# PEER sub-layer of a DeepNorm decoder layer: all first-table chunks before one pass over the second table, and the gate scatter as one fp32r product per token

## The chip, the cores and the metric

The kernel runs on one core of a Trainium2 chip, as one launch. The metric is the device time of an execution in microseconds (us). Each kernel was executed several times, and the median is given. One execution was also recorded by the hardware profiler, with the start and duration of each engine's instructions and DMA packets.

Engines are named as the profile names them: PE is TensorE (matrix products), PEld its weight loads, DVE is VectorE, ACT is ScalarE, SP is the sync engine, whose queue issues all loads and stores of this kernel. Every engine works off its own instructions in a fixed order.

## The reference, cut to what matters

One decoder layer over 256 tokens of width 2048, in fp32. A modulated layer norm, an attention mixture and an output projection come first; this change leaves them alone. The second sub-layer is PEER: each token scores two sets of 128 sub-keys with 8 heads, keeps 16 of the 128 x 128 pairs a head, and sums those 128 experts out of 16,384.

```python
def peer(h, w_pq, sub_key_1, sub_key_2, u_table, v_table):
    ...
    idx = i1 * PEER_N_KEYS + i2          # 8 heads x 16 experts per token
    g = jax.nn.softmax(vals, axis=-1)
    ...
        u = u_table[it]
        a = jnp.einsum('td,tkd->tk', ht, u)
        w = jax.nn.gelu(a.astype(jnp.float32), approximate=False).astype(ht.dtype) * gt
        return jnp.einsum('tk,tkd->td', w, v_table[it])

def reference(...):
    ...
        ffn = peer(h, w_pq[l], sub_key_1[l], sub_key_2[l], u_table[l], v_table[l])
        x = layer_norm(DN_ALPHA * x + g2 * ffn, ln2_g[l], ln2_b[l])
```

## The kernel before

The kernel gathers nothing. It computes the products with all 16,384 experts for all 256 tokens, applies GELU, multiplies by a dense gate matrix (zero where a token did not choose an expert) and multiplies by the whole second table. Both tables are streamed from HBM, 128 MB each.

Precision: an fp32 operand is split into `hi` (fp32r) and `lo` (the rest, fp32r), and a product is made of three fp32r products (`hi*hi`, `hi*lo`, `lo*hi`). `piece` (L92) loads one 1 MB piece of a table into one of three `raw` buffers by an SP queue DMA, and makes two half pieces: ACT casts `hi` (L98), DVE subtracts `lo` (L100). There are four `hi` and four `lo` buffers, so two pieces can stand ready ahead of PE. `prepare` asks for a piece ahead of its use.

The PEER part runs in stages, by the time of the profile:

- about 565 to 996 us: `u_chunk` (L781) for chunks 0 to 15 of the first table U. A chunk is four pieces and 512 experts. Per piece PE does 16 pairs of one matmul of 512 columns (L132, `hi_u` against `act` hi and lo together) and one of 256 (L133, `lo_u`). Every two pieces ACT and DVE add two PSUM banks into the chunk's `W` tile (L791, L792), and ACT applies GELU (L793). After each piece `pull(PULL_U[c])` lets the expert choice go on by a budget: `axis_top` and `pair_top` find the chosen experts on DVE, and `scatter` (L905) builds the gate matrix.
- about 996 to 1341 us: `v_half(0, 0)` multiplies W of chunks 0 to 15 with the matching rows of the second table V, into eight PSUM banks; the sums go to `y`.
- about 1341 to 1707 us: `u_chunk` for chunks 16 to 31, with the last `w_ada` rows and the residual beside it.
- about 1707 to 2054 us: `v_half(1, LATE)`. The last six rows of V come last, bank by bank, so that the last norm can start on finished columns.

The gate scatter, per token: a one-hot row of the first index, `o1`, and a one-hot row of the second index times the gate, `o2`, both fp32; their outer product sum is a 128 x 128 gate block:

```python
nc.vector.tensor_scalar(o2, iota, i2T[:, t:t + 1], gT[:, t:t + 1], op0=ALU.is_equal, op1=ALU.mult)
nc.tensor.matmul(ps[:, q * P:(q + 1) * P], o1[:, q, :], o2, start=True, stop=True)
```

Four tokens make a group and fill one PSUM bank, which ACT copies into `stg` (L928); every 16 tokens `stg` (1 MB) goes to DRAM as `g_d`. PE carries one fp32 matmul as two records of 128 columns. A group of `scatter` builds `o1` on ACT (four `Abs`, one `Relu`, L919 and L921) or on DVE (L917) by the list `on_vector`: none of four groups for tokens 0 to 127, two of four for tokens 128 to 255.

`v_weights(c)` (L983) loads the gates of two chunks (`gl`, 1 MB in runs of 512 bytes), multiplies W by them on DVE (L989) and splits the product into `whi` and `wlo` (L157, L158). There are 16 W buffers, so all 16 chunks of a half stay in SBUF.

The order on each engine is not that of the code alone: the framework sets it when the program is built, from priorities and its own durations. So the text below shows it from the built programs.

## Time and profile before

| | us |
|---|---|
| median of 3 runs (2072.44 to 2072.8) | 2072.49 |
| the profiled execution | 2069.06 |
| its span, first to last instruction | 2067.3 |
| PE busy in the span | 1999.3 (97%) |
| DVE busy | 1433.5 (69%) |
| ACT busy | 1027.1 (50%) |
| DMA queue of SP, share of 16 engines | 64.9% |

The table is from the head of the profile page. A matmul's record is longer than its distance to the next, since matmuls overlap in the array; so the cost of matmuls on PE's path is read from the starts of successive ones. Idle time of an engine is put down to what ended it. The DMA share is the mean busy share of the core's 16 DMA engines.

### The profile page before, as it was taken

The numbers are of one execution on the slowest core, as the hardware profiler recorded it, in microseconds if no ns is written. First come the engines' busy times: TensorE is split into PE (matmuls) and PEld (weight loads), VectorE is DVE, ScalarE is ACT, GpSimd is POOL, SyncE is SP. The second block draws the span as 40 slices with busy tenths as digits, with TensorE's granted clock in tenths as the row PEclk, the third lists the DMA queues.
The fourth block names the chain that finished last, engine by engine and source line by source line (L and its number), as shares of the span: only waits on it lengthen the run. The fifth ranks groups of instructions, "written<-read, shape, count | busy, mean of one in ns | idle before, by whom it ended". The sixth has DMA issues, their size and how long they took to land.

```text
span 2067.3 us, 26814 instructions
## 1 busy us (share of the span) xinstructions
PE 1999.3 (97%) x10328; PEld 1671.3 (81%) x10329; DVE 1433.5 (69%) x2510; ACT 1027.1 (50%) x1481; POOL 0.2 (0%) x4
## 2 busy tenths in 40 slices
PE   6999998989999999999999999999999999999997
PEld 3567686769988888998888888888888888888886
DVE  7589988889799677676765454477776555445457
ACT  2323457444554778876444444454444454444441
POOL 0000000000000000000000000000000000000000
PEclk8999999989999999999999999999999999999999
DMA  9788877858545555556985555578876656555552
GB/s 368 310 328 337 328 306 277 334 224 325 186 159 191 199 208 197 212 203 225 287 282 188 199 184 203 186 270 307 295 285 245 226 205 237 190 201 186 201 203 102
DMA packets 100865, 496.13 MB, mean 240 GB/s; under 512 B 7793, under 2 KB 41729, under 8 KB 42881
## 3 DMA queue, kind: packets, MB, share of 16 engines
q1 hardware_dynamic: 100736, 494.41, 64.9%
q8 instruction: 81, 1.33, 0.2%
q14 instruction: 48, 0.39, 0.1%
HBM read 473.40 MB, written 20.98 MB: 239 GB/s over the span
## 4 chain that ended last, share of the span: by engine, by line
PE 90%; DVE 7%; ACT 1%; DMA 1%; issue 1%; SPq 0%; DVEq 0%; ACTq 0%
PE u_ps L132 23%; PE u_ps L133 11%; PE v_ps L137 11%; PE v_ps L139 11%; PE v_ps L138 11%; PE win_ps L330 3%; PE g_ps L927 3%; DVE ada L208 2%; PE win_ps L138 2%; PE win_ps L139 2%; PE win_ps L137 1%; PE wo_ps L139 1%; PE wo_ps L138 1%; PE wo_ps L137 1%; PE wpq_ps L137 1%; PE wpq_ps L139 1%
## 5 line engine op out<-in xcount | busy, mean ns | idle before, releaser
L132 PE MATMUL u_ps<-act,hi_u 128*128 128x512 f32 x2048 | 726.5, 399 | 3.0 <-DVE W L792 3.0
L133 PE MATMUL u_ps<-act,lo_u 128*128 128x256 f32 x2048 | 573.6, 280 | 0.0
L100 DVE TENSOR_TENSOR lo_v<-raw_v,hi_v 128x1024 fp32r<-128x1024 f32 x244 | 297.9, 1224 | 263.4 <-ACT hi_v L98 263.3
L132 PEld LDWEIGHTS u_ps<-act,hi_u 128*128 128x128 f32 x2048 | 385.5, 188 | 94.8 <-DVE W L792 3.3
L100 DVE TENSOR_TENSOR lo_u<-raw_u,hi_u 128x1024 fp32r<-128x1024 f32 x256 | 312.2, 1222 | 179.2 <-ACT hi_u L98 178.6
L98 ACT CAST hi_v<-raw_v 128x1024 fp32r<-128x1024 f32 x244 | 257.2, 1054 | 327.8 <-PE v_ps L139 321.3
L133 PEld LDWEIGHTS u_ps<-act,lo_u 128*128 128x128 f32 x2048 | 387.1, 189 | 0.0
L137 PE MATMUL v_ps<-hi_v,whi 128*128 128x512 f32 x976 | 379.7, 389 | 0.0
L138 PE MATMUL v_ps<-lo_v,whi 128*128 128x512 f32 x976 | 379.7, 389 | 0.0
L139 PE MATMUL v_ps<-hi_v,wlo 128*128 128x512 f32 x976 | 379.7, 389 | 0.0
L98 ACT CAST hi_u<-raw_u 128x1024 fp32r<-128x1024 f32 x256 | 267.5, 1047 | 206.5 <-PE u_ps L132 187.0
L208 DVE SCALAR_TENSOR_TENSOR ada<-ada,cb 128x1024 f32<-128x1024 f32 x192 | 229.1, 1219 | 13.8 <-DMA ada<-in_w_ada_dram 13.5
L139 PEld LDWEIGHTS v_ps<-hi_v,wlo 128*128 128x128 f32 x976 | 183.2, 188 | 38.3
L138 PEld LDWEIGHTS v_ps<-lo_v,whi 128*128 128x128 f32 x976 | 183.2, 188 | 37.9
L137 PEld LDWEIGHTS v_ps<-hi_v,whi 128*128 128x128 f32 x976 | 183.2, 188 | 37.9
L925 DVE TENSOR_SCALAR o<-iota,i2T,gT 128x128 f32<-128x128 f32 x256 | 72.9, 342 | 20.0 <-PE g_ps L927 19.9
L330 PE MATMUL win_ps<-raw_win,hmod 128*128 128x512 f32 x192 | 85.6, 601 | 1.2 <-ACT hmod L301 1.2
L137 PE MATMUL wpq_ps<-act,hi_wpq 128*128 128x256 f32 x256 | 73.5, 290 | 2.3 <-ACT act L157 2.1
L791 ACT COPY W<-u_ps 128x256 f32<-128x256 f32 x128 | 47.2, 369 | 52.0 <-PE u_ps L133 51.6
L139 PE MATMUL wpq_ps<-act,lo_wpq 128*128 128x256 f32 x256 | 72.5, 285 | 0.5 <-DVE lo_wpq L100 0.5
L138 PE MATMUL wpq_ps<-act,hi_wpq 128*128 128x256 f32 x256 | 72.9, 286 | 0.0
L330 PEld LDWEIGHTS win_ps<-raw_win,hmod 128*128 128x128 f32 x192 | 36.3, 193 | 42.8 <-issue 41.0
(320 smaller groups left out, 2313.8 us busy)
## 6 DMA issues: line engine op xcount, KB each, us to landing
raw_u<-in_u_dram SPq DMA_DIRECT2D x128, 1024.0 KB, 4.8
raw_v<-in_v_dram SPq DMA_DIRECT2D x122, 1024.0 KB, 4.8
ada<-in_w_ada_dram SPq DMA_DIRECT2D x96, 1024.0 KB, 6.4
raw_win<-in_w_in_dram SPq DMA_DIRECT2D x32, 1024.0 KB, 8.9
raw_wo<-in_w_o_dram SPq DMA_DIRECT2D x16, 1024.0 KB, 6.8
raw_wpq<-in_w_pq_dram SPq DMA_DIRECT2D x16, 1024.0 KB, 6.5
g_d<-stg SPq DMA_DIRECT2D x16, 1024.0 KB, 4.9
gl<-g_d SPq DMA_DIRECT2D x16, 1024.0 KB, 6.7
```

The source lines that it names most:

```text
L98: nc.scalar.copy(hi, raw[:, 2 * j:2 * j + 2, :])
L100: nc.vector.tensor_sub(lo, raw[:, 2 * j:2 * j + 2, :], hi.bitcast(F32))
L132: nc.tensor.matmul(pss[e], hi[:, i, es], act[:, k], start=first and j == 0 and i == 0, stop=False)
L133: nc.tensor.matmul(pss[e][:, 1], lo[:, i, es], act_hi[:, k, :], start=False, stop=last and j == 1 and i == 3)
L137: nc.tensor.matmul(o, sh, mh, start=start, stop=False)
L138: nc.tensor.matmul(o, sh, ml, start=False, stop=False)
L139: nc.tensor.matmul(o, sl, mh, start=False, stop=stop)
L208: nc.vector.scalar_tensor_tensor(w[:, z, :], w[:, z, :], 1.0, cb[:, z * 1024:(z + 1) * 1024], op0=ALU.mult, op1=ALU.mult, accum_out=(modc, ...
L330: nc.tensor.matmul(ps[th], act[:, i, ts], src[:, i, :], start=i == 0, stop=i == 3)
L791: nc.scalar.copy(ws[:, e], pss[e][:, 1])
L925: nc.vector.tensor_scalar(o2, iota, i2T[:, t:t + 1], gT[:, t:t + 1], op0=ALU.is_equal, op1=ALU.mult)
L927: nc.tensor.matmul(ps[:, q * P:(q + 1) * P], o1[:, q, :], o2, start=True, stop=True)
```

## The change

**Order of the stages.** All 32 U chunks run first, then one pass over V in the order `V_ORDER`: chunks 24 to 31, then 0 to 23. The V sums stay in the eight PSUM banks for the whole pass; `y` goes, and the residual is taken from `x1` at the end. The last `w_ada` rows, the reload of `x1` and the rows of the last norm are moved from the second U loop into the V pass (or ahead of it).

**W through DRAM.** There are 8 W buffers (`RING`). Each of chunks 0 to 23 is stored to `w_d` after its GELU (512 KB, SP queue) and loaded again four chunks ahead of its use in the V pass. Chunks 24 to 31 stay.

**Scatter.** `gT` holds each gate as hi and lo in fp32r. `o1` is fp32r, `o2` holds the hi and the lo row side by side, and each token is one fp32r matmul of 256 columns. A group of four tokens needs two banks and two ACT copies. `stg` and `g_d` double (2 MB per 16 tokens); `v_weights` loads both halves and adds them on DVE. `o1` and `o2` of a group are made by whole-group DVE instructions with broadcast operands. DVE builds `o1` for one of four groups throughout.

**Budget.** `PULL_U` is 1.75 a piece for all chunks, and the costs that a group counts are 2.6 (with `o1` on DVE) or 1.9. So a chunk of four pieces pulls 7.0, or 7.0 / ((2.6 + 3 x 1.9) / 4) = 3.4 groups once the expert choice is done.

```diff
-PULL_U = (2.32, 2.23, 1.88, 1.67, 1.83, 2.15, 2.15, 2.41, 2.57, 2.53, 2.28, 2.75, 2.72, 3.19, 2.79, 3.42)
+RING = 8
+SPILL = 32 - RING
+V_ORDER = tuple(range(SPILL, 32)) + tuple(range(SPILL))
+PULL_U = 1.75
...
-    g_d = dram.tile([16, P, NKEY, 16], F32, name="g_d")
+    g_d = dram.tile([16, P, 2, NKEY, 16], F32, name="g_d")
+    w_d = dram.tile([SPILL, P, 4, T], F32, name="w_d")
...
-            return back.tile([P, 4, T], F32, tag=f"W{c % 16}", name=name)
+            return back.tile([P, 4, T], F32, tag=f"W{c % RING}", name=name)
...
+                    if kg == 0 or s < 63:
                         after = s + kg, 1 - kg
                         prepare(a["u"][after], "u{}_{}".format(*after))
+                    else:
+                        prepare(a["v"][4 * V_ORDER[0]], f"v{V_ORDER[0]}_0")
...
-                        pull(PULL_U[c])
+                        pull(PULL_U)
+            if c < SPILL:
+                nc.sync.dma_start(w_d[c], W[c])
...
-            gT = sel.tile([P, T], F32, name="gT")
+            gT = sel.tile([P, T, 2], F32R, name="gT")
...
-                nc.vector.tensor_copy(gT[:, ts], ps[:, 2 * P:3 * P])
+                nc.vector.tensor_copy(gT[:, ts, 0], ps[:, 2 * P:3 * P])
+                nc.vector.tensor_sub(gT[:, ts, 1], ps[:, 2 * P:3 * P], gT[:, ts, 0].bitcast(F32))
...
             def scatter(th, on_vector):
 
                 for tb in range(8 * th, 8 * th + 8):
-                    stg = sel.tile([P, NKEY, 16], F32, tag="stg", name=f"stg{tb}", bufs=2)
+                    stg = sel.tile([P, 2, NKEY, 16], F32, tag="stg", name=f"stg{tb}", bufs=2)
                     for b in range(4):
-                        ps = bank(("sm", "tr")[b % 2], f"g_ps{tb}_{b}")
-                        o1 = sel.tile([P, 4, P], F32, tag="o1", name=f"o1_{tb}_{b}", bufs=2)
+                        t0 = tb * 16 + b * 4
+                        four = slice(t0, t0 + 4)
+                        shp = [P, 4, P]
+                        io = iota.unsqueeze(1).broadcast_to(shp)
+                        o1 = sel.tile(shp, F32R, tag="o1", name=f"o1_{tb}_{b}", bufs=2)
                         vec = b in on_vector
-                        for q in range(4):
-                            t = tb * 16 + b * 4 + q
-                            if vec:
-                                nc.vector.tensor_scalar(o1[:, q, :], iota, i1T[:, t:t + 1], None, op0=ALU.is_equal)
-                            else:
-                                nc.scalar.activation(o1[:, q, :], iota, AF.Abs, bias=i1n[:, t:t + 1])
-                        if not vec:
-                            nc.scalar.activation(o1, o1, AF.Relu, bias=1.0, scale=-1.0)
-                        for q in range(4):
-                            t = tb * 16 + b * 4 + q
-                            o2 = sel.tile([P, P], F32, tag="o2", name=f"o2_{t}", bufs=4)
-                            nc.vector.tensor_scalar(o2, iota, i2T[:, t:t + 1], gT[:, t:t + 1], op0=ALU.is_equal,
-                                                    op1=ALU.mult)
-                            nc.tensor.matmul(ps[:, q * P:(q + 1) * P], o1[:, q, :], o2, start=True, stop=True)
-                        nc.scalar.copy(stg[:, :, b * 4:(b + 1) * 4], ps.rearrange("p (t i) -> p i t", t=4))
-                        yield 1.9 if vec else 1.1
+                        if vec:
+                            nc.vector.tensor_tensor(o1, io, i1T[:, four].unsqueeze(2).broadcast_to(shp), op=ALU.is_equal)
+                        else:
+                            dist = sel.tile(shp, F32, tag="dist", name=f"dist{tb}_{b}", bufs=1)
+                            for q in range(4):
+                                nc.scalar.activation(dist[:, q, :], iota, AF.Abs, bias=i1n[:, t0 + q:t0 + q + 1])
+                            nc.scalar.activation(o1, dist, AF.Relu, bias=1.0, scale=-1.0)
+                        eq = sel.tile(shp, F32, tag="eq", name=f"eq{tb}_{b}", bufs=1)
+                        nc.vector.tensor_tensor(eq, io, i2T[:, four].unsqueeze(2).broadcast_to(shp), op=ALU.is_equal)
+                        o2 = sel.tile([P, 4, 2, P], F32R, tag="o2", name=f"o2_{tb}_{b}", bufs=2)
+                        both = [P, 4, 2, P]
+                        nc.vector.tensor_mul(o2, eq.unsqueeze(2).broadcast_to(both),
+                                             gT[:, four, :].bitcast(F32).unsqueeze(3).broadcast_to(both))
+                        for j in range(2):
+                            ps = bank(("sm", "tr")[j], f"g_ps{tb}_{b}_{j}")
+                            for q in range(2):
+                                nc.tensor.matmul(ps[:, q * T:(q + 1) * T], o1[:, 2 * j + q, :],
+                                                 o2[:, 2 * j + q].rearrange("p z n -> p (z n)"), start=True, stop=True)
+                            t = b * 4 + 2 * j
+                            nc.scalar.copy(stg[:, :, :, t:t + 2], ps.rearrange("p (t z i) -> p z i t", t=2, z=2))
+                        yield 2.6 if vec else 1.9
                     nc.sync.dma_start(g_d[tb], stg)
...
-            later = puller(itertools.chain(axis_top(3), pair_top(0), mixed(pair_top(1), scatter(0, ()), 0.9),
-                                           scatter(1, (1, 3))))
-            for c in range(16):
+            later = puller(itertools.chain(axis_top(3), pair_top(0), mixed(pair_top(1), scatter(0, (1,)), 0.9),
+                                           scatter(1, (1,))))
+            for c in range(32):
                 u_chunk(c, later)
             later(1e9)
...
+            g2w = base.tile([P, 4, D], F32, tag="act", name="g2w")
...
+            def w_load(j):
+                c = V_ORDER[j]
+                if c < SPILL:
+                    W[c] = w_tile(c, f"Wl{c}")
+                    nc.sync.dma_start(W[c], w_d[c])
...
             def v_weights(c):
                 if c % 2 == 0:
-                    gates[0] = val.tile([P, 16, 8, 16], F32, tag="gl", name=f"gl{c}", bufs=1)
-                    nc.sync.dma_start(gates[0], g_d[:, :, 4 * c:4 * c + 8, :].rearrange("b p i t -> p b i t"))
+                    gates[0] = val.tile([P, 2, 16, 8, 16], F32, tag="gl", name=f"gl{c}", bufs=1)
+                    for z in range(2):
+                        nc.sync.dma_start(gates[0][:, z], g_d[:, :, z, 4 * c:4 * c + 8, :].rearrange("b p i t -> p b i t"))
+                    nc.vector.tensor_add(gates[0][:, 0], gates[0][:, 0], gates[0][:, 1])
                 i0 = c % 2 * 4
                 wv = W[c].rearrange("p i (b t) -> p b i t", b=16)
-                nc.vector.tensor_mul(wv, wv, gates[0][:, :, i0:i0 + 4, :])
+                nc.vector.tensor_mul(wv, wv, gates[0][:, 0, :, i0:i0 + 4, :])
...
+            pss = banks8("v_ps")
+            for j, c in enumerate(V_ORDER):
+                if j > 0:
+                    prev = whi, wlo
+                whi, wlo = v_weights(c)
+                if j + 4 < 32:
+                    w_load(j + 4)
+                for i in range(4):
+                    if 4 * j + i >= P - LATE:
+                        continue
+                    for jj, (hi, lo) in enumerate(piece(a["v"][4 * c + i], f"v{c}_{i}")):
+                        for th in range(2):
+                            ts = slice(th * P, (th + 1) * P)
+                            for n in range(2):
+                                mm3(pss[4 * th + 2 * jj + n], whi[:, i, ts], wlo[:, i, ts], hi[:, n, :], lo[:, n, :],
+                                    start=(j == 0 and i == 0), stop=False)
+                if 2 <= j < 18:
+                    m = G2 + j - 2
+                    w = g2w[:, j % 4, :].rearrange("p (z n) -> p z n", z=2)
+                    nc.sync.dma_start(w, a["w_ada"][m].rearrange("p (z n) -> p z n", z=2))
+                    for z in range(2):
+                        nc.vector.scalar_tensor_tensor(w[:, z, :], w[:, z, :], 1.0, cb[:, z * 1024:(z + 1) * 1024],
+                                                       op0=ALU.mult, op1=ALU.mult, accum_out=(modc, modh)[z][:, m:m + 1])
...
+                    nc.sync.dma_start(row_d.rearrange("(c p) -> p c", p=P), modc[:, G2:G2 + 16],
+                                      allow_slow_non_contiguous=True)
+                    bcast_row(g2b, row_d)
+                if j == 20:
+                    for th in range(2):
+                        nc.sync.dma_start(x1[:, th, :], x1_d[th])
+                    for z, nm in enumerate(("ln2_g", "ln2_b")):
+                        bcast_row(rows[:, z, :], a[nm])
...
+            late = base.tile([P, 2, 2, 2, 2, 512], F32R, tag="act", name="late")
...
-                yt = y[:, th]
+                yt = x1[:, th]
...
-                    nc.vector.tensor_add(yt[:, cs], yt[:, cs], tmp)
+                    nc.vector.scalar_tensor_tensor(yt[:, cs], yt[:, cs], ALPHA, tmp, op0=ALU.mult, op1=ALU.add)
```

What the built programs show, row by row (engine's own order; `u27` is step 27 of U, half a chunk, `v27_2` piece 2 of chunk 27; `hi_u29_1_0` is half 0 of piece 1 of step 29).

PE, at the end of a U piece late in the scatter of before; `g_ps13_0` and `g_ps13_1` are two groups of four tokens, of whose eight rows the last five stand here:

```order
L927 MATMUL g_ps13_0_8479<-o2_211_8495,o1_13_0_8480 128x128
L927 MATMUL g_ps13_1_8499<-o2_212_8505,o1_13_1_8500 128x128
L927 MATMUL g_ps13_1_8499<-o2_213_8508,o1_13_1_8500 128x128
L927 MATMUL g_ps13_1_8499<-o2_214_8511,o1_13_1_8500 128x128
L927 MATMUL g_ps13_1_8499<-o2_215_8514,o1_13_1_8500 128x128
L132 MATMUL u_ps27_0_8433<-act_73,hi_u27_1_0_8469 128x512
L133 MATMUL u_ps27_0_8433<-act_73,lo_u27_1_0_8471 128x256
```

PE, at the end of a U piece of the changed kernel (both pieces of step 29 are done); one group of four tokens in two banks:

```order
L135 MATMUL u_ps29_1_7943<-act_73,hi_u29_1_1_7982 128x512
L136 MATMUL u_ps29_1_7943<-act_73,lo_u29_1_1_7984 128x256
L942 MATMUL g_ps5_1_0_8060<-o2_5_1_8058,o1_5_1_8054 128x256 x2
L942 MATMUL g_ps5_1_1_8064<-o2_5_1_8058,o1_5_1_8054 128x256 x2
L135 MATMUL u_ps30_0_8070<-act_73,hi_u30_0_0_8041 128x512
L136 MATMUL u_ps30_0_8070<-act_73,lo_u30_0_0_8043 128x256
```

Four matmuls of 256 columns stand where four (or, with two groups, eight) fp32 matmuls of 128 stood; a group stands at the end of a piece as before.

DVE, where the operands of that same group `5_1` are made in the changed kernel; `W14 <- u_ps28` is the sum of the finished step 28:

```order
L934 TENSOR_TENSOR eq5_1_8056<-iota_3934,i2T_3942 128x512
L103 TENSOR_TENSOR lo_u29_0_0_7912<-raw_u29_0_7908,hi_u29_0_0_7910 128x1024
L103 TENSOR_TENSOR lo_u29_0_1_7916<-raw_u29_0_7908,hi_u29_0_1_7914 128x1024
L103 TENSOR_TENSOR lo_u29_1_0_7980<-raw_u29_1_7976,hi_u29_1_0_7978 128x1024
L798 TENSOR_TENSOR W14_7831<-W14_7831,u_ps28_0_7832 128x256
L927 TENSOR_TENSOR o1_5_1_8054<-iota_3934,i1T_3941 128x512
L103 TENSOR_TENSOR lo_u29_1_1_7984<-raw_u29_1_7976,hi_u29_1_1_7982 128x1024
L798 TENSOR_TENSOR W14_7831<-W14_7831,u_ps28_1_7833 128x256
L937 TENSOR_TENSOR o2_5_1_8058<-eq5_1_8056,gT_3943 128x1024
```

The operands of the group are finished behind the sum of step 28, while PE uses the group behind step 29.

SP, in the first V pass of before, at chunks 2 and 3; `gl` is a gate load:

```order
L82 DMA raw_v2_0_9425<-in_v_dram 128x2048
L986 DMA gl10_10554<-g_d_75 128x16x128
L82 DMA raw_v2_1_9459<-in_v_dram 128x2048
L82 DMA raw_v2_2_9493<-in_v_dram 128x2048
L986 DMA gl12_10838<-g_d_75 128x16x128
```

SP, in the V pass of the changed kernel, at chunks 27 to 29 (the fourth to sixth of its order):

```order
L85 DMA raw_v27_2_12470<-in_v_dram 128x2048
L1012 DMA gl0_13133<-g_d_75 128x16x128
L85 DMA raw_v27_3_12504<-in_v_dram 128x2048
L1042 DMA g2w_11964<-in_w_ada_dram 128x2048
L85 DMA raw_v28_0_12552<-in_v_dram 128x2048
L1006 DMA Wl4_13142<-w_d_76 128x1024
L85 DMA raw_v28_1_12586<-in_v_dram 128x2048
L1042 DMA g2w_11964<-in_w_ada_dram 128x2048
L85 DMA raw_v28_2_12620<-in_v_dram 128x2048
```

Between the V pieces the queue now also carries the second gate half, the stored W and the `w_ada` rows. From the load of `raw_v27_0` to just before that of the first piece of chunk 4 (nine chunks later) the built program has 36 V pieces, 11 gate halves, 10 `w_ada` rows (1 MB each) and 9 W tiles (512 KB).

## Rows read from the trace of the kernel before

**Rows 1.** Two stretches: start:end, length; each engine's busy us; PEclk, DMA share, GB/s
```profile
800.00:979.00 179.00, 179.00 (x1139) 161.53 (x1138) 126.27 (x317) 134.16 (x265) 0.00 (x0) 1.00 0.60 211
...
1715.00:2050.00 335.00, 335.00 (x1480) 277.39 (x1479) 181.61 (x168) 142.76 (x138) 0.00 (x0) 1.00 0.52 188
```

**Rows 2.** The page, engines and costliest groups: busy, mean ns, idle before
```profile
PE 1999.3 (97%) x10328; PEld 1671.3 (81%) x10329; DVE 1433.5 (69%) x2510; ACT 1027.1 (50%) x1481; POOL 0.2 (0%) x4
...
L132 PE MATMUL u_ps<-act,hi_u 128*128 128x512 f32 x2048 | 726.5, 399 | 3.0 <-DVE W L792 3.0
```

**Rows 3.** Groups by line, 600 to 1000 us: busy, mean ns, idle before
```profile
L98 ACT CAST hi_u<-raw_u 128x1024 fp32r<-128x1024 f32 x117 | 122.1, 1047 | 77.7 <-PE u_ps L132 73.6 <-ACT hi_u L98 2.4 <-issue 1.1
L925 DVE TENSOR_SCALAR o<-iota,i2T,gT 128x128 f32<-128x128 f32 x256 | 72.9, 342 | 20.0 <-PE g_ps L927 19.9
L927 PE MATMUL g_ps<-o,o 128*128 128x128 f32 x512 | 66.9, 280 | 0.0
L919 ACT ACTIVATE o<-iota,i1n 128x128 f32<-128x128 f32 x192 | 63.8, 398 | 0.0
...
L928 ACT COPY stg<-g_ps 128x512 f32<-128x512 f32 x64 | 37.4, 585 | 0.4 <-PE g_ps L927 0.4
L921 ACT ACTIVATE o<-o 128x512 f32<-128x512 f32 x48 | 30.2, 629 | 0.8
...
L791 ACT COPY W<-u_ps 128x256 f32<-128x256 f32 x62 | 22.8, 368 | 11.5 <-PE u_ps L133 11.5
L793 ACT ACTIVATE W<-W 128x512 f32<-128x512 f32 x31 | 19.5, 629 | 22.5 <-DVE W L792 22.4
```

**Rows 4.** Groups by line, 1010 to 1330 us, then 1345 to 1690 us
```profile
L989 DVE TENSOR_TENSOR W<-W,gl 128x1024 f32<-128x1024 f32 x10 | 12.1, 1222 | 14.6 <-DMA gl<-g_d 14.6
...
L1031 DVE TENSOR_TENSOR y<-y,cb 128x2048 f32<-128x2048 f32 x2 | 4.6, 2284 | 0.0
```

**Rows 5.** The tail in order of time, after the last matmul
```profile
2055.05 0.69 DVE L1070 TENSOR_TENSOR fin_t<-v_ps,cb 128x512 f32<-128x512 f32 x1 [1.79 <-PE v_ps L139]
```

**Rows 6.** The chain that ended last, its scatter steps: start us, us
```profile
679.10 0.89 PE g_ps L927 x8
685.55 0.89 PE g_ps L927 x8
...
904.30 1.92 PE g_ps L927 x16
911.88 1.92 PE g_ps L927 x16
```

**Rows 7.** Stretches of U without scatter, first and second loop
```profile
600.00:670.00 70.00, 70.00 (x405) 61.19 (x404) 69.35 (x215) 36.04 (x48) 0.00 (x0) 1.00 0.52 184
1350.00:1520.00 170.00, 170.00 (x965) 147.50 (x964) 127.27 (x159) 82.76 (x107) 0.00 (x0) 1.00 0.80 292
```

**Rows 8.** PE in order of time, around eight tokens: start us, us
```profile
830.02 2.08 PE L927 MATMUL g_ps<-o,o 128*128 128x128 f32 x16
831.86 0.48 PE L132 MATMUL u_ps<-act,hi_u 128*128 128x512 f32 x1
832.17 0.28 PE L133 MATMUL u_ps<-act,lo_u 128*128 128x256 f32 x1
```

**Rows 9.** PE in order of time, fp32r matmuls of 256 columns
```profile
559.92 0.28 PE L139 MATMUL wpq_ps<-act,lo_wpq 128*128 128x256 f32 x1
560.04 0.28 PE L137 MATMUL wpq_ps<-act,hi_wpq 128*128 128x256 f32 x1
```

**Rows 10.** The page, DMA issues: KB each, median us to landing
```profile
raw_u<-in_u_dram SPq DMA_DIRECT2D x128, 1024.0 KB, 4.8
...
gl<-g_d SPq DMA_DIRECT2D x16, 1024.0 KB, 6.7
```

**Rows 11.** Two stretches dense with gate traffic, columns as in Rows 1
```profile
1030.00:1062.00 32.00, 32.00 (x143) 26.50 (x142) 21.21 (x19) 13.21 (x14) 0.00 (x0) 1.00 0.85 280
...
979.00:996.00 17.00, 17.00 (x98) 14.76 (x97) 12.36 (x13) 9.64 (x12) 0.00 (x0) 1.00 0.97 309
```

64 lines of the change are left out of this document (15 added, 49 removed).

## The prediction

> **What bounds the kernel now.** I read the page first, then stretches of U and V, then PE in order of time. From the first U chunk on PE is never idle: in a stretch of U with scatter and one of V it is busy for the whole stretch at PEclk 1.00, the 2.4 GHz level [rows 1], and of 2048 pairs of U only one waited, 3.0 us behind a DVE sum [rows 2]. DVE waited 14.6 us for gate loads and ACT for DVE, and PE noticed none of it [rows 3, 4]. So the end of the program is a sum of PE's matmuls, plus the last norm, whose chain starts when DVE, idle for 1.79 us, gets the last bank [rows 5]. The reader should see two things: a matmul taken from PE after 590 us comes off the end at its full start-to-start distance, and work on other engines costs nothing until it makes PE wait.
>
> **Removed: the fp32 scatter matmuls.** In the chain, the steps that hold four tokens (20 of them) come 6.45 us apart, which is a U piece plus the four tokens; the 22 others hold eight [rows 6]. A piece is 16 pairs; 405 records in 70 us make 0.3457 us a pair and 5.53 a piece [rows 7], so four tokens cost 0.92. For eight, PE goes from 830.02 to 831.86, and the pair behind it takes 0.31 from its first to its second start where others take 0.23: 1.84 + 0.08 = 1.92 [rows 8]. Sum: 20 x 0.92 + 22 x 1.92 = 60.6 us for 256 tokens.
>
> **Added: 256 fp32r matmuls of 256 columns.** Before has no scatter matmul of that form. The nearest row is the fp32r product of the query projection, with 256 columns and its own weight load each: 0.12 us apart [rows 9]. 256 x 0.12 = 30.7. From below it is bounded by half a 512-column matmul of V, 335 us / 1480 / 2 = 0.113 [rows 1], or 29.0; from above by the fp32 token's own 0.24, or 61.4, if something in the new form (weights freshly made by ACT or DVE, say) held it there. I take 0.12, because it is the same form on the same engine. **Net: -29.9, bounds -31.6 to +0.8.**
>
> The Trainium skill (TensorE: Matmul & The Clock Gate, section "Wait — 56ns, not 53.3ns?") gives a warm matmul N / 2.4 GHz plus about 2.5 ns, 109 ns for 256 columns. By that the added work would be 28.0 us and the net -32.6. Rows 9 show 120 ns for this form, so page and trace differ here and the trace decides.
>
> **The pace of the pairs.** The second U loop runs at 170 us / 965 records, 0.3523 us a pair, not 0.3457 [rows 7]. I see no cause: same buffers, same clock. Either pace holds for hundreds of pairs. If the 1024 pairs of the second loop ran at the first loop's pace, 6.8 us would go; if the 590 fast pairs or so of the first loop ran at the slow one, 3.8 would come. With a group after most pieces both will be seen, as in the scatter of before. I take -1.5, bounds -6.8 to +3.8.
>
> **Moved at no cost.** The joins between U and V are already dense, so running one V pass instead of two halves gives PE nothing back; eight PSUM banks hold the sums as they did for half. The `y` copies and two DVE sums of 2.28 us [rows 4] leave engines that PE did not wait for. The 3.0 us wait of rows 2 lies where the DVE order is still the same, so I leave it (bounds -3 to +3). The last norm has one scaled sum in place of a sum, 0.69 us as before [rows 5].
>
> **ACT in U.** This is the cover that could go. A chunk needs 8 casts x 1.047 + 4 copies x 0.368 + 2 GELUs x 0.629 = 11.1 us. A group needs three times in four 4 x 63.8 / 192 + 0.629 = 1.96 us, and two copies x 0.585 instead of one: 2.64 [rows 3]. With 3.4 groups a chunk that is 9.0, so 20.1 us of ACT in a chunk that PE takes 64 x 0.349 + 3.4 x 0.48 = 24.0 us for: 84%, against 75% in the stretch from 800 to 979 [rows 1]. It fits. The copy now writes runs of two tokens where it wrote four; no row has that. From below 0.585; from above twice that, 1.17, where ACT just fills the chunk (20.1 + 6.8 x 0.585 = 24.1). I take 0.585, since with runs of four 512 elements cost no more than the contiguous 512 of GELU, 0.629.
>
> **DVE.** A group needs a comparison of 512 elements (0.69 by the nearest row of that size [rows 5]), a product of 1024 (1.22 [rows 4]) and in one of four another comparison: 2.1 us, against at least 4 x 0.342 = 1.37 before [rows 3]. But there is one group a piece, not two. Before, 2.7 us of 7.5; now about 1.8 us of 6. In V it gains 16 sums of 2.28 us and 32 `w_ada` products: per two chunks (43.4 us) 2.28 + 4 x 1.22 = 7.2 us, on 54% [rows 1]; about 71%. Fits.
>
> The new waits: in the DVE order shown, group `5_1` waits for the sum of step 28. Behind that sum stand 0.69 + 1.22 us, the second half of the sum (256 columns, no longer than the 0.69) and 1.22, at most 3.8 us, while PE has two pieces and a group, 11.5 us, before it wants the operands. Some 7.5 us are to spare. On SP, the store of W waits for GELU, and the loads of U pieces queue behind it; they would wait anyway for a `raw` buffer, and a load lands in 4.8 us [rows 10] while five pieces of 5.5 us are buffered ahead.
>
> **DMA in V.** In the nine chunks counted in the SP order there are 61.5 loads of 1 MiB, 64.5 MB, in 9 x 96 x 0.226 = 195 us: 330 GB/s. The queue has not sustained that here. Scaled to a full share, the stretches with gate loads give 280 / 0.85 = 329 and 309 / 0.97 = 319 [rows 11], that with few gives 292 / 0.80 = 365 [rows 7]; gate halves are 18% of the bytes, so I expect about 350 and a share of 0.94. From above, at 319, 202 us would be needed: 7 us of PE waiting. I take +0, as three raw buffers and two split pieces stand ahead.
>
> The Trainium skill (DMA: Bandwidth & Descriptors, section "Specifications") calls 512 bytes enough for line rate. By that a gate half would cost what a V piece does, and the share would be 330 / 365 = 0.90. Rows 10 have 6.7 us to landing against 4.8 for the same bytes, so the trace does not bear it out; the sum is the same.
>
> **Sum.** -29.9 - 1.5 = -31.4 us. The profiled execution of 2069.06 us (span 2067.3 and 1.8 around it) becomes 2037.7. It lay 3.4 us below the median; the median becomes 2072.5 - 31.4 = 2041.1.
>
> **Rivals.**
>
> *Small waits eat part of it.* DMA in the nine chunks (up to 7 us), a late `o2`, late gate sums in DVE's queue. For it: 330 GB/s is beyond what was held for long. Against it: the depth ahead of PE. It gives 2046 to 2062, say 2048. Chance 0.20.
>
> *ACT becomes the bound of U: slower.* The two copies of a group write runs of two elements. If such a copy took 1.76 us (three times the row), ACT would need 20.1 + 6.8 x 1.17 = 28.1 us in a chunk of 24.0, and the 19 chunks that the 64 groups fill would lose 4.1 each, 78 us; with the 31.4 gained, 2119. It decides from about 1.4 us a copy: there the loss is 1.65 us a chunk, 31 in all. Against it: rows 3 show no price of scattered writes. Chance 0.09.
>
> *The matmul is no cheaper.* If the fp32r form took 0.24 us a token, the time is 2072.5 + 0.8 - 1.5 = 2072. Rows 9 speak against it. Chance 0.05.
>
> *More than forecast.* All pairs at the fast pace and the wait of 3.0 us gone: -29.9 - 6.8 - 3.0, 2033 or below. Chance 0.06.
>
> **How the numbers follow.** The forecast, 2034 to 2046, has the remaining 0.60, so 2041. Leaving out 2 in 10, the range is 2033 to 2060: it drops the slower rival, the one without gain, and the far ends. A measurement of this kernel can tell about 0.2%, 4 us, from no change. Faster by more: 0.60 + 0.20 + 0.06 = 0.86; the same 0.05; slower 0.09.
>
> **What would show it.** Right: PE busy for the whole of U and V; scatter matmuls 0.12 us apart, four to a group; copies of 0.6 us; a DMA share near 0.94 early in V. Wrong: gaps in U before scatter matmuls that end with ACT or DVE; `hi` casts that no longer wait for PE (ACT full); gaps in V that end with `raw_v`; scatter matmuls 0.24 us apart.

## The result, and the profile after

The changed kernel takes 2045.01 us, the median of 4 runs (2043.28 to 2047.66), against 2072.64 us of before beside it (2072.44 to 2074.71). The ratio is 0.9872, with a 95% interval of 0.9859 to 0.9885: 27.6 us less, where 31.4 was forecast. The profiled execution took 2044.22 us, with a span of 2042.4.

The head of the page and three of its costliest groups (busy us, mean ns, then idle time of the engine just before them) stand against [rows 2]:

```profile
PE 1973.8 (97%) x10072; PEld 1644.3 (81%) x10072; DVE 1497.3 (73%) x2344; ACT 1048.2 (51%) x1538; POOL 0.2 (0%) x4
...
L136 PE MATMUL u_ps<-act,lo_u 128*128 128x256 f32 x2048 | 575.1, 281 | 0.9 <-DVE lo_u L103 0.9
...
L141 PE MATMUL v_ps<-lo_v,whi 128*128 128x512 f32 x976 | 380.0, 389 | 2.3 <-DVE lo_v L103 2.3
L140 PE MATMUL v_ps<-hi_v,whi 128*128 128x512 f32 x976 | 379.9, 389 | 1.0 <-DVE W L798 1.0
```

PE still sets the end. The 3.0 us wait of [rows 2] is gone, 0.9 us stand in its place, and 3.3 us of waits are new in V, where before had none.

Where the time went is read from PE in order of time (start us, us): the first matmul of U, the first and last of V. The changed kernel, then before, which has two U loops and two V halves:

```profile
574.75 0.40 PE L135 MATMUL u_ps<-act,hi_u 128*128 128x512 f32 x1
...
1328.92 0.40 PE L140 MATMUL v_ps<-hi_v,whi 128*128 128x512 f32 x1
...
2029.72 0.39 PE L142 MATMUL v_ps<-hi_late,wlo 128*128 128x512 f32 x1
```

```profile
571.90 0.40 PE L132 MATMUL u_ps<-act,hi_u 128*128 128x512 f32 x1
...
996.53 0.40 PE L137 MATMUL v_ps<-hi_v,whi 128*128 128x512 f32 x1
...
1344.71 0.39 PE L132 MATMUL u_ps<-act,hi_u 128*128 128x512 f32 x1
...
1706.62 0.40 PE L137 MATMUL v_ps<-hi_v,whi 128*128 128x512 f32 x1
...
2054.62 0.39 PE L139 MATMUL v_ps<-hi_late,wlo 128*128 128x512 f32 x1
```

The differences of these starts give the stages. The same was done for every run below; the label of each run is named again where its experiment is told. All times are us, of one profiled execution each.

| profiled execution | ahead of U | U | V | behind V | span |
|---|---|---|---|---|---|
| before | 571.9 | 424.6 + 361.9 = 786.5 | 348.2 + 348.0 = 696.2 | 12.7 | 2067.3 |
| the changed kernel | 574.8 | 754.2 | 700.8 | 12.7 | 2042.4 |
| again | 574.5 | 751.5 | 701.0 | 12.7 | 2039.7 |
| row_runs | 575.1 | 751.8 | 698.1 | 12.9 | 2037.8 |
| sums_first | 569.9 | 753.5 | 706.5 | 12.7 | 2042.7 |
| rows_and_sums | 574.3 | 751.8 | 696.1 | 12.9 | 2035.0 |
| old_scatter | 574.2 | 776.3 | 702.1 | 12.7 | 2065.3 |
| old_scatter_rows | 574.6 | 776.4 | 696.1 | 12.8 | 2059.9 |
| order_hllh | 574.6 | 750.4 | 700.6 | 12.7 | 2038.3 |
| mends_hllh | 574.3 | 750.9 | 696.8 | 12.9 | 2034.9 |
| mends_hhll | 575.0 | 749.9 | 696.1 | 12.8 | 2033.9 |
| first_pull | 575.2 | 753.8 | 697.4 | 12.7 | 2039.1 |
| mends_small | 574.4 | 753.9 | 698.8 | 12.9 | 2039.9 |
| dense_scatter | 573.7 | 755.0 | 702.0 | 12.8 | 2043.4 |

From before to after: U -32.4, V +4.6, ahead of U +2.9, together -24.8 in the profiled pair. The medians differ by 27.6, and U and V alone make -32.4 + 4.6 = -27.8. That close a fit is partly chance: U of the same changed program was 2.7 us shorter in a second profile (`again`).

The waits of PE by what ended them (us in all, times, the longest), from the first U matmul on, and four stretches of the changed kernel with the columns of [rows 1]: U with scatter, early V, and two pieces of V 10 us long together:

```profile
PE v_ps L141 <- DVE lo_v L103: 2.3, 2, 1.8
PE v_ps L140 <- DVE W L798: 1.0, 2, 0.5
PE u_ps L136 <- DVE lo_u L103: 0.9, 3, 0.5
```

```profile
800.00:979.00 179.00, 179.00 (x1052) 157.74 (x1052) 127.86 (x146) 126.93 (x226) 0.00 (x0) 1.00 0.71 263
...
1400.00:1550.00 150.00, 150.00 (x664) 124.19 (x663) 112.28 (x109) 64.64 (x62) 0.00 (x0) 1.00 0.94 331
```

```profile
1585.00:1590.00 5.00, 5.00 (x23) 4.13 (x22) 5.00 (x5) 1.97 (x2) 0.00 (x0) 1.00 0.82 213
1590.00:1595.00 5.00, 5.00 (x23) 4.13 (x22) 3.87 (x4) 2.62 (x4) 0.00 (x0) 1.00 0.70 49
```

ACT is busy for 126.9 of 179 us in U, 71%, DVE for 112.3 of 150 us in early V, 75%, and the DMA share there is 0.94: the covers held. But in one stretch of 5 us the DMA engines moved 49 GB/s where the 150 us from 1400 us on have 331. SP's queue in order of time has the new write of the g2 modulation row just ahead of it:

```profile
1583.26 0.33 SPq L85 DMA_DIRECT2D raw_v<-in_v_dram  x1
1583.64 0.43 SPq L1048 DMA_DIRECT2D row_d<-modc  x1
1584.12 4.94 SPq L81 DMA_DIRECT2D ln_rows<-in_ln_g_dram  x1
```

This write takes the 2048 values from 128 partitions of 16 columns each, one 4-byte run a value. In the kernel before, `spread_row` had PE transpose them first, in a PSUM bank; in the one V pass all eight banks hold sums. There it was one write of 512-byte runs, and it took 1.4 us to land.

The groups of the scatter by line, 690 to 1240 us (busy us, mean ns, idle before), stand against [rows 3]:

```profile
L937 DVE TENSOR_TENSOR o<-eq,gT 128x1024 fp32r<-128x1024 f32 x64 | 78.3, 1223 | 33.3 <-PE g_ps L942 33.3
L945 ACT COPY stg<-g_ps 128x512 f32<-128x512 f32 x128 | 72.1, 623 | 0.0
...
L942 PE MATMUL g_ps<-o,o 128*128 128x256 f32 x256 | 41.1, 283 | 0.0
```

From the start of one scatter matmul to the next matmul it is 0.120 us on average, 30.8 us in all 256. PE waited for none of them.

At the join of U and V, DVE in order of time (start us, us, in brackets the idle time before and what ended it) and PE's two gaps:

```profile
1328.47 2.29 DVE L1013 TENSOR_TENSOR gl<-gl 128x2048 f32<-128x2048 f32 x1 [2.76 <-DMA gl<-g_d]
1330.68 1.22 DVE L103 TENSOR_TENSOR lo_v<-raw_v,hi_v 128x1024 fp32r<-128x1024 f32 x1
1331.82 0.41 DVE L798 TENSOR_TENSOR W<-W,u_ps 128x256 f32<-128x256 f32 x1
1332.15 1.22 DVE L1016 TENSOR_TENSOR W<-W,gl 128x1024 f32<-128x1024 f32 x1
1333.28 0.41 DVE L798 TENSOR_TENSOR W<-W,u_ps 128x256 f32<-128x256 f32 x1
```

```profile
1332.28 0.50 PE L140 MATMUL v_ps<-hi_v,whi 128*128 128x512 f32 x1 [0.47 <-DVE W L798]
...
1333.75 0.50 PE L140 MATMUL v_ps<-hi_v,whi 128*128 128x512 f32 x1 [0.50 <-DVE W L798]
```

DVE waits 2.76 us for a gate load, adds the gate halves for 2.29 us, and only then comes to the two sums that free the last PSUM banks of U, for which PE waits.

### The profile page after: what moved, and what is told of

Same layout as the page of the kernel before. It is cut to its first block, busy times and chain, and to the rows that moved or that the text cites. A ratio compares the mean times of both kernels' runs of the same rounds, so it can differ in the third digit from the quotient of the medians.

```text
span 2042.4 us, 26235 instructions
## 1 busy us (share of the span) xinstructions
PE 1973.8 (97%) x10072; PEld 1644.3 (81%) x10072; DVE 1497.3 (73%) x2344; ACT 1048.2 (51%) x1538; POOL 0.2 (0%) x4
## 4 chain that ended last, share of the span: by engine, by line
PE 85%; DVE 9%; DMA 3%; ACT 2%; issue 1%; SPq 0%; DVEq 0%; ACTq 0%
PE u_ps L135 21%; PE u_ps L136 11%; PE v_ps L141 10%; PE v_ps L140 10%; PE v_ps L142 10%; PE win_ps L334 3%; DVE ada L212 2%; PE win_ps L141 2%; DMA gl<-g_d 2%; PE win_ps L142 2%; PE g_ps L942 2%; PE win_ps L140 1%; PE wo_ps L142 1%; PE wo_ps L141 1%; PE wo_ps L140 1%
## 5 line engine op out<-in xcount | busy, mean ns | idle before, releaser
L136 PE MATMUL u_ps<-act,lo_u 128*128 128x256 f32 x2048 | 575.1, 281 | 0.9 <-DVE lo_u L103 0.9
L212 DVE SCALAR_TENSOR_TENSOR ada<-ada,cb 128x1024 f32<-128x1024 f32 x160 | 191.0, 1218 | 9.9 <-DMA ada<-in_w_ada_dram 9.8
L937 DVE TENSOR_TENSOR o<-eq,gT 128x1024 fp32r<-128x1024 f32 x64 | 78.3, 1223 | 33.3 <-PE g_ps L942 33.3
L799 ACT ACTIVATE W<-W 128x512 f32<-128x512 f32 x64 | 40.7, 636 | 73.4 <-DVE W L798 73.4
L101 ACT CAST hi_win<-raw_win 128x1024 fp32r<-128x1024 f32 x40 | 40.9, 1049 | 61.4 <-PE win_ps L142 30.8
## 6 DMA issues: line engine op xcount, KB each, us to landing
gl<-g_d SPq DMA_DIRECT2D x32, 1024.0 KB, 10.1
```

The source lines that it names most:

```text
L101: nc.scalar.copy(hi, raw[:, 2 * j:2 * j + 2, :])
L136: nc.tensor.matmul(pss[e][:, 1], lo[:, i, es], act_hi[:, k, :], start=False, stop=last and j == 1 and i == 3)
L212: nc.vector.scalar_tensor_tensor(w[:, z, :], w[:, z, :], 1.0, cb[:, z * 1024:(z + 1) * 1024], op0=ALU.mult, op1=ALU.mult, accum_out=(modc, ...
L799: nc.scalar.activation(ws, ws, AF.Gelu)
L937: nc.vector.tensor_mul(o2, eq.unsqueeze(2).broadcast_to(both), gT[:, four, :].bitcast(F32).unsqueeze(3).broadcast_to(both))
```

## The experiments

Three theories stood before these runs: the scatter's form is worth some 29 us whatever the order of stages; V's 4.6 us come from two things that the change moved (the 4-byte row write, the gate sum at the join) and not from the demand of 330 GB/s; the pace of U's pairs and the wait at 586 us are matters of order, not of cost. Each quoted paragraph is what was expected before the run, with its rival.

### Again

No edit (`again` in the table).

> The changed kernel once more, on the chip that also runs the three others of this set. Theory: the 27.6 us between the medians are 32.4 less in U, 4.6 more in V, and nothing in the stages ahead of U; that these took 2.85 us more in the profiled execution is chance. Then the same three gaps of PE return (1.3 us at the join of U and V, 2.2 us some 40 us behind the write of the modulation row, 0.9 us later), U takes 754 us and V 701, and the first U matmul comes anywhere from 571 to 575 us. Rival: the gaps are chance; then V takes 697 to 699 us here.

2042.76 us (2040.06 to 2045.89), with before at 2071.9 on this chip. U took 751.5 us, V 701.0, and the same gaps returned: two at the join, one some 40 us behind the row write and one 83 us after that, 1.7 and 1.6 us from start to start. So V's loss is no chance. U is 2.7 us shorter than in the first profile though the program is the same, and U's first matmul comes at 574.5. Over all runs of this table it comes at 569.9 to 575.2, with the code ahead of U the same in all of them but for buffers; so the 2.9 us there lie within what one kernel varies by. Before was profiled once, so more can't be said of its own spread.

### The row write in longer runs

The run `row_runs`, cut to the write:

```diff
-nc.sync.dma_start(row_d.rearrange("(c p) -> p c", p=P), modc[:, G2:G2 + 16], allow_slow_non_contiguous=True)
+flip = val.tile([P, 32], F32, name="flip")
+nc.vector.transpose(flip, modc[:, G2 - 16:G2 + 16])
+runs = row_d.rearrange("(c b q) -> b c q", b=4, q=32)
+for b in range(4):
+    nc.sync.dma_start(runs[b], flip[32 * b + 16:32 * b + 32, :])
```

> Only the write of the g2 modulation row differs: DVE transposes it in blocks of 32 x 32, and it goes to DRAM in 64 runs of 128 bytes rather than 2048 of 4 bytes. Theory A (the 4-byte write empties the DMA engines for some 10 us and the V pieces never catch up): no stretch of 49 GB/s is left, the gaps of 2.2 and 0.9 us go, V takes 697.7 us, the time falls by 3.1 us. Rival B (the loads of the first half of V are simply too many for the queue): the gaps stay, perhaps at other places, and the time is the same within 1 us.

2040.98 us (2039.63 to 2041.75), V 698.1, and the gaps behind the write are gone: theory A. The medians differ by 1.8 us where 3.1 was expected, and the executions of the two kernels overlap, so what shows the gain is V (2.9 us less than in `again`) and the missing gaps. The page's DMA part for 17 us from the write's issue on (packets and MB moved; then the kind of transfer, KB each, median us from issue to landing), of the changed kernel and of this one:

```profile
DMA packets 2446, 2.84 MB, mean 167 GB/s; under 512 B 2100, under 2 KB 2100, under 8 KB 2100
...
row_d<-modc SPq DMA_DIRECT2D x1, 8.0 KB, 13.7
```

```profile
DMA packets 924, 5.19 MB, mean 305 GB/s; under 512 B 207, under 2 KB 277, under 8 KB 315
...
row_d<-flip SPq DMA_DIRECT2D x4, 2.0 KB, 6.2
```

The 8 KB cost 2.35 MB of other loads, 6 to 7 us of the queue at 365 GB/s. PE, with pieces ahead, notices a part of it, at 1627 us, 43 us after the write was issued. It does not notice it in every run: in `first_pull` below the same 4-byte write takes 13.0 us, and PE has no gap behind it. The Trainium skill (DMA: Bandwidth & Descriptors, section "Specifications") puts the least size for line rate at 512 bytes; the trace agrees for 4-byte runs, with 13.7 us for 8 KB, and the prediction had applied that section to the gate loads only. The mend uses what another page of the Trainium skill (VectorE: DVE Perf Modes, section "The three transpose paths") states, that DVE transposes blocks of 32 x 32. Here that leaves runs of 128 bytes, which was enough.

### The sums first

The run `sums_first`; `tc.issue_after` fixes the order of two instructions on DVE.

```diff
-nc.vector.tensor_add(ws[:, e], ws[:, e], pss[e][:, 0])
+last_sum[0] = nc.vector.tensor_add(ws[:, e], ws[:, e], pss[e][:, 0])
...
-nc.vector.tensor_add(gates[0][:, 0], gates[0][:, 0], gates[0][:, 1])
+with (tc.issue_after(last_sum[0].ins) if c == 30 else ExitStack()):
+    nc.vector.tensor_add(gates[0][:, 0], gates[0][:, 0], gates[0][:, 1])
```

> Only one thing differs: on DVE the sum of the gate halves for chunks 30 and 31 is put behind the last PSUM sums of U. Theory: at the join PE waited because these sums stood behind that gate sum, which waited 2.8 us for its load; then the two gaps there (1.3 us together) go and the time falls by 1.3 us. Rival: the sums are late for another reason (ACT's copies ahead of them); then the gaps stay.

2044.77 us (2039.19 to 2047.26), against 2042.76 of `again` on the same chip: no gain. The gaps at the join did go, as the theory had it, but V took 706.5 us. Behind the hole that the row write leaves in the loads PE now waited 6.4 us in three waits, where it was 2.3 and 2.6 us in the two profiles of the changed kernel. That PE came sooner to the hole is the likely reason, not a shown one. Behind the two longer waits (3.4 and 2.2 us) the granted clock fell; around the first of them (columns of [rows 1]):

```profile
1619.00:1624.00 5.00, 1.59 (x7) 1.05 (x6) 3.79 (x3) 1.05 (x1) 0.00 (x0) 1.00 1.02 425
1624.00:1626.00 2.00, 2.00 (x8) 1.60 (x7) 2.00 (x3) 0.00 (x0) 0.00 (x0) 0.74 0.79 213
1626.00:1628.00 2.00, 2.00 (x7) 1.54 (x6) 2.00 (x2) 0.25 (x1) 0.00 (x0) 0.50 0.90 377
```

Matmuls that are 0.227 us apart at 2.4 GHz were 0.427 apart at 1.2 GHz, eight in a row here and six behind the second wait. So a mend of one wait was paid back by the next ones, with a surcharge.

### Both mends

The two edits above together (`rows_and_sums`).

> Both mends together: the row write in 64 runs of 128 bytes, and the gate sum for chunks 30 and 31 behind the last PSUM sums of U. Theory: what V lost is these two and nothing else, so PE has no gap of over 0.4 us from the join to the end, V takes 696.2 us as the two halves of before did together, and the time is 4.6 us under the changed kernel's, 2038 to 2041. Rival: with PE earlier at the join the loads fall behind elsewhere (the 330 GB/s demand), and gaps of 1 to 6 us come back at other places.

2036.58 us (2032.72 to 2038.85; ratio 0.9826, 0.9803 to 0.9848). V takes 696.1 us as before's two halves did, and this is all that PE waited from U's start on:

```profile
PE u_ps L136 <- DVE lo_u L103: 0.9, 3, 0.5
```

Early V still has the demand that the changed kernel has there:

```profile
1400.00:1550.00 150.00, 150.00 (x663) 124.22 (x662) 113.36 (x111) 65.10 (x63) 0.00 (x0) 1.00 0.94 334
```

So in this order the demand as such costs nothing: the two moved steps were the whole loss in V. Two runs below, with other budgets, show that it is near the limit: there a gate sum in the middle of V meets a late load.

### The scatter of before in the new order

The changed kernel with the loop of `scatter` as it was before (`old_scatter`: fp32 one-hots of a token at a time, one bank and one copy a group), `g_d` and `gl` single, no gate sum. The core of it:

```diff
-nc.tensor.matmul(ps[:, q * T:(q + 1) * T], o1[:, 2 * j + q, :], o2[:, 2 * j + q].rearrange("p z n -> p (z n)"), ...)
+nc.tensor.matmul(ps[:, q * P:(q + 1) * P], o1[:, q, :], o2, start=True, stop=True)
```

> The changed kernel with the scatter of before: fp32 one-hot rows of one token at a time, fp32 matmuls of 128 columns, one bank and one copy a group, single gates in DRAM. Order of stages, W through DRAM and the late rows stay as changed. Theory A (the scatter's form is all of the gain): U is longer by 29.4 us (256 tokens x 0.235 against 256 x 0.12), and V shorter by 1 to 2 us with half the gate loads: 2045 + 28 = 2073. Rival B (running U in one piece and V in one pass gave a good part): the time is well below 2065.

2066.06 us (2063.63 to 2067.75): 23 us above the changed kernel beside it, not 28. U is 776.3 us, 22 to 25 longer. The products behave as expected: their starts take 54.4 us against 30.8, and the pairs behind the groups 4.4 us more in all. What was not expected is that most pairs now keep the faster pace: of some 2000 that stand apart from groups and waits, some 300 run at 353.3 ns, against some 860 to 1160 in the two profiles of the changed kernel. At 6.6 us for a thousand that gives back 4 to 6 us. V has one wait of 2.9 us after the row write, and behind it a granted clock of 0.50 for 4 us. The same with the row write mended (`old_scatter_rows`):

> The scatter of before in the new order of stages, now with the row write in 64 runs of 128 bytes. Theory: the terms add. V takes 696.2 us as with both mends (there is no gate sum here), U 776 as with the old scatter before, so the time is 6 us under that run, 2060, and the scatter's form is worth 23 to 24 us against the kernel with both mends: 29 less for the products, and 5 back because after the fp32 groups most pairs stay at the fast pace. Rival: the 4-byte write was not what cost V its time in this order; then V stays near 702.

2061.83 us (2060.99 to 2062.21), U 776.4, V 696.1, PE's waits the same single row as above. The terms add. With the scatter as in before the rest of the change, so mended, is worth 11 us (2072.9 to 2061.8), nearly all of it in U. But that is not shown to be the worth of the new order of stages. Six to seven us of it are pace: in the one profile of before the last 1080 pairs or so all ran at 353.3 ns, here the last 730 or so all at 346.7, and which pace such a long stretch has can change from one execution of a program to the next, as the following section shows. Some 2 us more are the wait of 3.0 us with its clock, which goes with the budget of the first chunks.

### The order of the U products

The run `order_hllh`:

```diff
+if i % 2 == 0:
     nc.tensor.matmul(pss[e], hi[:, i, es], act[:, k], ...)
     nc.tensor.matmul(pss[e][:, 1], lo[:, i, es], act_hi[:, k, :], ...)
+else:
+    nc.tensor.matmul(pss[e][:, 1], lo[:, i, es], act_hi[:, k, :], ...)
+    nc.tensor.matmul(pss[e], hi[:, i, es], act[:, k], ...)
```

> Only the order of the U products differs: hi, lo, lo, hi for two steps of the contraction in place of hi, lo, hi, lo. Theory: the two paces of the pairs (346.7 and 353.2 ns) are two rhythms of the alternation of 512 and 256 columns that a disturbance switches; with the order changed there is one rhythm, at 226.7 + 120 = 346.7 ns a pair, since V's 512 columns take 226.7 and the query projection's 256 columns take 120. Then U falls by 900 to 1160 slow pairs x 6.5 ns = 6 to 7.5 us. Rival: the pace is set by something in the data's place (buffers, banks); then both paces are still there and U is the same within 2 us.

2037.85 us (2037.18 to 2040.12). U is 750.4 us, 1 to 4 less, not 6 to 7.5. There is one rhythm, as the theory had it, but at 348.3 ns a pair: over four pairs the starts are 233, 236, 116, 113, 232, 231, 113 and 119 ns apart. The same 70 us behind the scatter, in the changed kernel's first profile, in its second, and with this order (the number in brackets behind PE's busy time counts matmul records; one or two lie on an edge):

```profile
1240.00:1310.00 70.00, 70.00 (x398) 60.70 (x397) 47.32 (x47) 34.20 (x44) 0.00 (x0) 1.00 0.93 316
```

```profile
1240.00:1310.00 70.00, 70.00 (x406) 61.72 (x405) 48.25 (x48) 36.12 (x47) 0.00 (x0) 1.00 0.92 316
```

```profile
1240.00:1310.00 70.00, 70.00 (x404) 61.08 (x403) 45.34 (x45) 35.09 (x45) 0.00 (x0) 1.00 0.93 317
```

One program runs this stretch at 353.3 ns a pair in one execution and at 346.7 in another. V's 700.6 us still have the row write in 4-byte runs: PE waits 3.0 us in three waits, 100 to 130 us after that write, and not at the join. With both mends, hi, lo, lo, hi is `mends_hllh` and hi, hi, lo, lo is `mends_hhll`:

> Both mends of V (row write in runs of 128 bytes, gate sum behind the PSUM sums) and the order hi, lo, lo, hi of the U products. Theory (the terms add, since they lie in different stages): V 696.1 us as with the mends, U 750 us, 348.3 ns for every pair; the time is 1 to 2 us under that of the mends alone, about 2035. Rival: the other order's gaps in early U eat it; then the time equals that of the mends alone, 2036.6.

> Both mends, and the U products as hi, hi, lo, lo. Theory: with hi, lo, lo, hi the products of a kind already stand in twos, with weights of different steps, and one rhythm of 348.3 ns a pair resulted; this order alternates in the same twos, so one rhythm again, 346.7 to 348.5, U within 1 us of 750. Rival: two weight loads of one half piece stand closer together here, some show, and the pair goes to 353 or beyond; then U is 760 us or more.

2035.87 us (2035.12 to 2037.22; ratio 0.9824, 0.9810 to 0.9837) and 2035.48 us (2034.32 to 2036.71; 0.9821, 0.9806 to 0.9836), U 750.9 and 749.9, both at 348.3 ns a pair. Both medians are under the mends alone by about 1 us, which is within the spread of these runs; they are the lowest found, 7 to 10 us under the changed kernel's 2042.8 and 2045.0.

### The budget of the first chunks

The run `first_pull`:

```diff
-PULL_U = 1.75
+PULL_U = (2.32, 2.23, 1.88, 1.67, 1.83, 2.15) + (1.75,) * 26
```

> Only the budget of the first six U chunks differs: 2.32, 2.23, 1.88, 1.67, 1.83, 2.15 a piece as before, in place of 1.75. Theory: the 3.0 us wait at 586 us went because a smaller budget puts less of the expert choice ahead of the PSUM sums on DVE; with the old budget it comes back, 3 us and a stretch at a lower clock behind it, and the three gaps at 613 to 623 us go. U is longer by 2 to 4 us. Rival: the wait was chance, or it went with something else; then U stays at 751 to 754 us with its gaps at 613 to 623.

2040.86 us, a single execution. The wait came back, with a low clock behind it, and the three gaps at 613 to 623 us went. PE's waits, and the stretch behind the first of them; then the stretch behind the same wait in the kernel before:

```profile
PE u_ps L135 <- DVE W L798: 3.0, 1, 3.0
PE v_ps L141 <- DVE lo_v L103: 0.8, 1, 0.8
```

```profile
593.00:598.00 5.00, 5.00 (x16) 4.23 (x16) 5.00 (x27) 1.56 (x2) 0.00 (x0) 0.50 0.40 134
```

```profile
590.00:594.00 4.00, 4.00 (x16) 3.43 (x15) 4.00 (x21) 1.56 (x2) 0.00 (x0) 0.57 0.30 92
```

So the budget of the first chunks decides it, as the theory had it, but not by the way that it named, a shorter stretch of choice on DVE. The rows of before, of this run and of the changed kernel: `sc_ps` are eight score products of the expert choice on PE, and the DVE row is the first PSUM sum of U's step 0.

```profile
583.99 1.05 PE L829 MATMUL sc_ps<-sk,qT 128*128 128x128 f32 x8
...
589.00 0.41 DVE L792 TENSOR_TENSOR W<-W,u_ps 128x256 f32<-128x256 f32 x1
...
589.46 0.50 PE L132 MATMUL u_ps<-act,hi_u 128*128 128x512 f32 x1 [3.02 <-DVE W L792]
```

```profile
587.25 1.05 PE L837 MATMUL sc_ps<-sk,qT 128*128 128x128 f32 x8
```

```profile
591.66 0.41 DVE L798 TENSOR_TENSOR W<-W,u_ps 128x256 f32<-128x256 f32 x1
...
592.40 1.05 PE L837 MATMUL sc_ps<-sk,qT 128*128 128x128 f32 x8
```

Counted from U's first matmul, the sum starts at 17.1 us in before and in this run and at 16.9 in the changed kernel: DVE is as late there, and PE does not wait. What moved are the score products, from 12.1 us, just ahead of U's step 1, to 17.6, in the middle of it. By the kernel's text `sc_ps` and `u_ps` share four PSUM banks, and a step of U takes two. With the score products ahead of step 1, PE does the eight matmuls of the step's first bank and then waits for the sum that frees a bank of step 0. That fits before, this run, the changed kernel and `mends_small` below; which bank each product got is not in the traces, so this part is argued.

U, 753.8 us, lies within the changed kernel's 751.5 to 754.2, since here only some 700 of 2030 pairs ran at the slower pace: the wait cost some 5 us with its clock (3.0, and eight pairs at 0.64 instead of 0.35), and pace and missing gaps gave most of that back. In V this run had no gap at the join and none behind the row write at 1583 us, but one of 1.2 us from start to start at 1473 us. DVE in order of time there has the pattern of the join again: a gate sum waits 6.04 us for its load, and the subtraction that PE needs stands behind it.

```profile
1470.83 2.29 DVE L1013 TENSOR_TENSOR gl<-gl 128x2048 f32<-128x2048 f32 x1 [6.04 <-DMA gl<-g_d]
1473.04 2.35 DVE L103 TENSOR_TENSOR lo_v<-raw_v,hi_v 128x1024 fp32r<-128x1024 f32 x2
```

Then the other way, with both mends (`mends_small`):

```diff
+PULL_U = (1.3,) * 4 + (1.75,) * 28
```

> Both mends, and a budget of 1.3 instead of 1.75 a piece in the first four U chunks. Theory: the three gaps of PE at 613 to 623 us (periods of 0.6, 0.85 and 0.6 us, 1.4 us in all over the usual 0.23) stand behind expert choice on DVE, as the 3.0 us wait of before did; a smaller budget takes them away, U falls by 1.4 us, and the scatter ends some 5 to 10 us later, still in U. Rival: the choice is on the path to the scatter's start, or other gaps come in; then U is the same or longer.

2039.99 us (2037.36 to 2041.82), 3.4 above the mends alone. A miss: the three gaps went, but a wait of 1.9 us for a DVE sum came at 600 us, followed by a stretch at 0.51 of the clock, and the waits at the join were back:

```profile
PE u_ps L135 <- DVE W L798: 1.9, 1, 1.9
PE v_ps L140 <- DVE W L798: 1.5, 2, 1.0
```

The scatter ends 24 us later than with both mends alone, at 1250 us instead of 1226, and the gate loads come later with it. At the join a gate sum that had waited 3.25 us for its load stands on DVE ahead of the last PSUM sums again. It is the third of V, that for chunks 28 and 29, and the edit binds only the fourth, for chunks 30 and 31. (In `first_pull` the scatter ends at 1207 us, all four gate sums come before the join, and PE has no gap there.) At 600 us the eight score products now stand just ahead of U's step 2, and the wait comes eight matmuls behind them, as in before a step earlier. So a smaller budget is not by itself better. What these runs point to is where the score products fall between the steps of U.

### A dense scatter

The run `dense_scatter`:

```diff
-PULL_U = 1.75
+PULL_U = (1.75,) * 8 + (4.15,) * 24
```

> Only the budget from chunk 8 on differs: 4.15 a piece in place of 1.75, so two groups of four tokens come behind each piece, as in 22 of 42 steps before, and the scatter is over after some 24 to 30 pieces more. Theory A (the spread is needed): a group takes both small PSUM banks, so the second group of a piece waits for two ACT copies of 0.6 us, about 1.2 us each time, and U is longer by 20 to 35 us. Rival B: the copies are done while PE works on the first group's pairs, or the order puts a piece between the groups, and U stays within 3 us.

2045.21 us, a single execution, U 755.0: nearer to rival B. The scatter is over at 989 us instead of 1227. The built program put 44 groups by themselves and only 20 in twos, so two groups behind every piece, as theory A had them, were not tried. PE in order of time:

```profile
928.54 0.63 PE L942 MATMUL g_ps<-o,o 128*128 128x256 f32 x4
...
936.99 1.11 PE L942 MATMUL g_ps<-o,o 128*128 128x256 f32 x8
```

Four matmuls of U waited about 0.5 us each, and the starts of the scatter matmuls take 32.1 us where the changed kernel has 30.8. V has a gap of 2.8 us at 1473 us, where a gate load is late as in `first_pull`, and one of 1.4 us 41 us behind the row write. Spreading the scatter over all of U is not what the gain rests on.

## Why the prediction was right, and where it was not

- **The bound.** Right. PE is busy for the whole of both long stretches, and U's and V's lengths in the profiles account for the change of the medians to 0.2 us, which is closer than two profiles of one program agree.
- **The scatter matmuls, -29.9.** Right. Removed were 56.7 us of starts plus 3.5 us in the pairs behind the groups, 60.2 where 60.6 was worked out. Added were 256 x 0.120 = 30.8, where 30.7 was taken from [rows 9]. Net -29.4. The 0.109 us that the prediction worked out from the Trainium skill (TensorE: Matmul & The Clock Gate, section "Wait — 56ns, not 53.3ns?") would have made it 28.0. The runs have 0.120 for this form as well, so they differ from that rule.
- **The pace, -1.5.** Right in size, in part by luck: the pairs apart from gaps and groups came out about 1 us shorter in the first profile and about 3 in the second, since one program has both paces, in other places from one execution to the next. That both paces would be seen was right too. No cause was named; the runs show two rhythms and what switches them (below), not what makes them.
- **The 3.0 us wait, left at 0.** The step that failed is the reason: "where the DVE order is still the same". DVE's sum did come as late as before (16.9 us into U, 17.1 before), but the budget of the first six chunks is smaller, 1.75 instead of 2.32 in the first, and with it the score products on PE moved from ahead of step 1 into it; `first_pull` shows that the old budget alone brings the wait back. Its price was short as well: before, five pairs or so ran at 1.2 GHz behind it. Gaps and clock together are about 2 us less in U than before.
- **Moved at no cost.** Wrong, and the largest miss: +4.6 us where 0 was taken. Two things that came with the new order were not counted by what they do in their place. The row write had been a write of 512-byte runs by way of PE and became 2048 runs of 4 bytes in the busiest stretch of the queue. The gate sum, which the prediction counted as DVE time in V (it had DVE at 71%, the trace 75%), stands in DVE's queue ahead of the sums that free PSUM at the join, and itself waits for a load. `row_runs`, `sums_first` and `rows_and_sums` show both, and with both mended V is back at 696.1 us, so nothing else is left.
- **DMA in V, 0.94 and +0.** Right: 0.94, and with the mends no wait, though with little to spare: a gate half now lands in 10.1 us (median of the page), where [rows 10] had 6.7 for the same size. The rival of small waits named the demand as its main price and late gate sums as another; the latter were one part of it. The demand alone cost nothing in this order.
- **ACT and DVE.** Right: copies of 0.623 us where 0.585 was taken, ACT at 71 to 76% in U (151.4 us of the 200 from 1000 us on), never the bound. The slower rival fell with its copy of 1.4 us or more.
- **The sum.** -31.4 against -27.6. The missing 3.8 us are V's 4.6, and some 0.5 each by which scatter and pace fell short, less about 2 for the wait of before that went. So two errors of opposite sign brought the forecast nearer than its steps deserve.
